# Feed forward: raw blocks of up and of the down projection in chunks of the large pool, only gate in the staging tiles, and the down sums in other PSUM banks

## The chip, the cores and the metric

The kernel runs on one core of one Trainium2 chip. The metric is device time in microseconds (us), from the start to the end of one execution. Lower is better.

## What is computed

Three residual blocks on one sequence of 512 rows with a model width of 1024. The first mixes attention and a gated delta rule; the second and the third are two layers of attention and feed forward (FFN). The change touches only the FFN, which runs once in each of these two layers:

```python
D_MODEL = 1024; SEQ = 512; D_FF = 2816; DEPTH_2 = 2

def swiglu_ffn(h, w_gate, w_up, w_down):
    g = jnp.einsum('bsd,df->bsf', h, w_gate)
    u = jnp.einsum('bsd,df->bsf', h, w_up)
    return jnp.einsum('bsf,fd->bsd', jax.nn.silu(g) * u, w_down)

def second_block(x, ...):
    for i in range(DEPTH_2):
        ...
        x = x + swiglu_ffn(rms_norm_2(x, ffn_norm[i]), w_gate[i], w_up[i], w_down[i])
    return x
```

Everything is float32. The width D_FF of 2816 is 22 blocks of 128 columns.

## The kernel before, in words

**Numbers.** Each float32 operand of a matmul is split into a rounded part (float32r) and a remainder: ScalarE casts the rounded part (`hi`), VectorE subtracts it from the original (`lo`), in `split` (L315). A product is then three matmuls, hi x hi, hi x lo, lo x hi (`mm3`). So a weight block has to be loaded, cast on ScalarE and subtracted on VectorE before TensorE has all that it needs. In the trace these are `whi` (L318) and `wlo` (L321).

**Tiling.** `ffn` (L2043) goes over 22 units, one for each block of 128 columns of gate and up. All activations lie feature first, so a result is 128 features x 512 rows.
- Units 0 to 3 are `plain`: gate (`pg`) and up (`pu`) are each 24 matmuls of 512 columns.
- Units 4 to 21 (`unit`) get gate and up together from 7 Strassen-like products instead of 8, each of 12 matmuls of 256 columns, into halves of three PSUM banks `sx`, `sy`, `sz`. `weights` (L2115) makes their stationary operands: gate itself for products 1 and 2, the sum of up's two halves (`s`, rounded `s1h` and `s1l`) for 5, a combination of gate and up for 6 and 3, and a difference made in up's own tile for 7 and 4. Product 4 of a unit is left pending, and issued in the next unit (`rest`). The products are issued in the order 1, 5, 4 of the unit before, 2, 6, 3, 7. The FFN's hidden block `m` is then split into `mh` and `ml` (`keep`).
- Units 4 to 19 carry a "fill" each: a part of the down projection. It takes 4 hidden blocks and two blocks of output features, 12 matmuls of 512 columns each into a bank `pd`; an add on VectorE (L600) then brings the sum into the residual `x`. The first half of a fill stands behind products 5 and 4, the second behind 6. The fill of unit 4 is issued ahead of its products.
- `down(16)` does the rest of the down projection, 8 x 18 matmuls.

**Memory.** Raw weights come through two staging tiles of 128 x 1024 (pool `wst`, tile name `st`). In a filled unit three loads go through them: gate (L2120), up (L2124), and the two halves of the down block (L2157). The rounded pairs `whi`, `wlo` have three places each, and every fourth pair goes into a place of its own. Chunks of 128 x 512 come from the pool `big` (57 places), which holds the activations, the hidden blocks and `s1`, `s1h`, `s1l`. PSUM has two banks of kind `acc`, five of kind `z` and one `o`; `sx` and `pd` use `acc`, `sy` and `sz` use `z`.

**What sets the order.** SyncE (SP) issues the loads. A scheduler at build time writes each engine's instructions in a fixed order: it goes by the order of the code, with the loads and the splits of `weights` and `fill` raised by a fixed priority (`high_priority`). A tile that is asked for waits until the last reader of its place is done. Since SP works through its own list in order, a load that waits for a place holds up all loads behind it. On TensorE a small driver (`Driver`) decides when the code goes from one stream to another; `self.free["acc"]` and `self.free["z"]` are its counts of free banks, which `release` returns.

Of the kernel before, what the change touches and what calls it, by code (L numbers as in the profile page):

```python
# [9 lines left out]
F32 = mybir.dt.float32  # L10
# [3 lines left out]
ALU = mybir.AluOpType  # L14
# [3 lines left out]
P = 128  # L18
T = 512
D = 1024  # L20
NC8 = 8
DFF = 2816
NFF = 22
# [145 lines left out]
class Net:  # L169
# [1873 lines left out]
    def ffn(self, x, R, l, nxt):  # L2043
# [11 lines left out]
        nc, ins, drv = self.nc, self.ins, self.drv  # L2055
# [35 lines left out]
        def plain(c, raw):  # L2091
            hh, ee = (R.h, R.ev) if raw else (h, ev_h)
            sg = self.work("sg")

            def evac_g(ps):
                if raw:
                    nc.vector.tensor_tensor(sg, ps, self.rfm, op=ALU.mult)
                    nc.scalar.activation(out=sg, in_=sg, func=AF.Silu)
                    nc.vector.tensor_tensor(sg, sg, self.rfm, op=ALU.mult)
                else:  # L2100
                    nc.scalar.activation(out=sg, in_=ps, func=AF.Silu)

            def evac_u(ps):
                m = self.work("m")
                nc.vector.tensor_tensor(m, ps, sg, op=ALU.mult)
                keep(c, m)
            yield from self.proj_fm([(ins["w_gate_2"][NFF * l + c], 8)], hh, evac_g, "pg", ee)
            yield from self.proj_fm([(ins["w_up_2"][NFF * l + c], 8)], hh, evac_u, "pu", ee)

        def keep(c, m):  # L2110
            mid[0][c], mid[1][c] = self.chunk(f"mh{c}", F32R), self.chunk(f"ml{c}", F32R)
            self.split(mid[0][c], mid[1][c], m)
            drv.set(evs[c], 2.5)

        def weights(c):  # L2115

            tt = lambda o, p, q, op: nc.vector.tensor_tensor(o, p, q, op=op)  # L2117
            with self.tc.high_priority(offset=self.woff):
                g = self.wst.tile([P, 1024], F32, tag="st", name="st")
                nc.sync.dma_start(out=g, in_=ins["w_gate_2"][NFF * l + c])  # L2120
                gh, gl = self.wpair()
                self.split(gh, gl, g)
                u = self.wst.tile([P, 1024], F32, tag="st", name="st")
                nc.sync.dma_start(out=u, in_=ins["w_up_2"][NFF * l + c])  # L2124
                s1 = self.chunk("s1")
                tt(s1, u[:, :T], u[:, T:], ALU.add)
                sh, sl = self.chunk("s1h", F32R), self.chunk("s1l", F32R)
                self.split(sh, sl, s1)

                tt(u[:, :T], g[:, :T], u[:, :T], ALU.subtract)  # L2130
                tt(g[:, :T], s1, g[:, :T], ALU.subtract)
                tt(g[:, T:], g[:, T:], g[:, :T], ALU.subtract)
                ch, cl = self.wpair()
                self.split(ch, cl, g)
                uh, ul = self.wpair()
                self.split(uh, ul, u)
            return {1: (gh, gl, 0), 2: (gh, gl, T), 5: (sh, sl, 0), 6: (ch, cl, 0), 3: (ch, cl, T),
                    7: (uh, ul, 0), 4: (uh, ul, T)}

# [12 lines left out]
        def fill(g, c):  # L2152

            with self.tc.high_priority(offset=self.woff):
                st = self.wst.tile([P, 1024], F32, tag="st", name="st")
                for i in range(2):
                    nc.sync.dma_start(out=st[:, T * i:T * i + T], in_=ins["w_down_2"][NC8 * l + c + i][:, T * g:T * g + T])  # L2157
                hi, lo = self.wpair()
                self.split(hi, lo, st)

            def one(i):
                yield self.free["acc"]
                acc = self.bank("acc", "pd")
                for j in range(4):
                    yield evs[4 * g + j]
                    cc = slice(T * i + j * P, T * i + (j + 1) * P)
                    self.mm3(acc, (hi[:, cc], lo[:, cc]), (mid[0][4 * g + j], mid[1][4 * g + j]), j == 0, j == 3)
                    yield 0
                part_x(c + i, acc)
                drv.release(self.free["acc"], 1.5)  # L2170
            return [one(0), one(1)]

        def unit(c, pending, fills):

            add = lambda o, p, q: nc.vector.tensor_tensor(o, p, q, op=ALU.add)  # L2175
            if fills and not pending:
                fills = fill(*fills)
                while fills:
                    yield from fills.pop(0)
            w = weights(c)  # L2180
            if fills:
                fills = fill(*fills)
# [64 lines left out]

        def stream():
            for c in range(4):
                yield from plain(c, c < RAW_UNITS)  # L2250
            pending = None
            for c in range(4, NFF):
                g = c // 4 - 1
                pending = yield from unit(c, pending, (g, 2 * (c % 4)) if g < 4 else None)
            yield from down(16, pending)
        drv.run([self.s_raw_end(R, tm=False), operands(), stream()])


# [109 lines left out]
```

## Time and profile before

| | |
|---|---|
| median of 3 runs | 2182.99 us (2180.08 to 2188.91) |
| the profiled execution's own time | 2191.84 us |
| its span in the profile | 2190.0 us |
| mean granted TensorE clock | 0.984 of full speed |
| busy share of the span | TensorE 96%, weight loads 85%, VectorE 67%, ScalarE 51%, GpSimd 5% |
| data moved | 181.93 MB, mean 83 GB/s |

The profile is of one execution; the times are of others. "Busy" for TensorE (PE) means that at least one matmul is under way. PEld are weight loads into TensorE, which overlap with matmuls; DVE is VectorE, ACT is ScalarE, POOL is GpSimd, SPq the queue of DMA issues on SyncE. `L302` is the line of the matmul in a helper that all products use, so groups on TensorE are told apart by their tiles.

### The profile page before, as it was taken

Reading aid. Unit: us, or ns where it says so; the run is one execution under the profiler, and the core shown is the slowest. Engines: PE = TensorE matmul, PEld = TensorE weight load, DVE = VectorE, ACT = ScalarE, POOL = GpSimd, SP = SyncE. Lnnn points to the kernel's source line nnn. Section 1 sums busy time; section 2 is a strip of 40 time slices with the busy share of each in tenths; the row PEclk is TensorE's granted clock in tenths of the full one; section 3 lists DMA queues with packets and bytes.
Section 4 is the critical chain, followed back from the end, with each engine's and each line's share of the span. In section 5 each row is a group of like instructions: output and inputs, shape, how many; then the busy total and the mean of one; then the engine's idle time right before and its main releaser. Section 6 shows DMA issues by size and latency. Waiting matters only on the chain.

```text
span 2190.0 us, 36607 instructions
## 1 busy us (share of the span) xinstructions
PE 2094.3 (96%) x14510; PEld 1851.3 (85%) x14510; DVE 1457.2 (67%) x2947; ACT 1112.6 (51%) x2227; POOL 117.2 (5%) x157
## 2 busy tenths in 40 slices
PE   7999999989999998999999999999999989999999
PEld 6798888879788877788878889988999877988887
DVE  8865865886442556755557777776677768766664
ACT  6556647555622355666655444444556644443432
POOL 2000100100000000000000000000111100000000
PEclk9999999999999999999999999999999999999999
DMA  4221121222334443011112233324211112232233
GB/s 157 70 81 50 46 74 50 59 80 64 100 101 140 149 156 104 20 49 49 58 47 89 75 100 102 101 87 118 76 59 59 59 53 73 90 104 87 90 94 106
DMA packets 78619, 181.93 MB, mean 83 GB/s; under 512 B 24688, under 2 KB 25328, under 8 KB 78448
## 3 DMA queue, kind: packets, MB, share of 16 engines
q1 hardware_dynamic: 77168, 175.40, 25.8%
q0 software_dynamic: 1280, 4.20, 0.6%
q8 instruction: 114, 1.87, 0.4%
q14 instruction: 57, 0.47, 0.1%
HBM read 170.13 MB, written 9.44 MB: 82 GB/s over the span
## 4 chain that ended last, share of the span: by engine, by line
PE 60%; DVE 20%; ACT 7%; DMA 6%; issue 3%; POOL 2%; SPq 0%; ACTq 0%; POOLq 0%; DVEq 0%
PE po L302 8%; PE pd L302 8%; PE pg L302 6%; DVE wlo L321 5%; PE sx L302 4%; PE pb L302 4%; ACT whi L318 3%; PE pz L302 3%; PE z L302 3%; PE pv L302 3%; PE sz L302 2%; DMA st<-w_up 2%; DMA st<-w_down 2%; PE wS L302 2%; DVE cacc L850 2%
## 5 line engine op out<-in xcount | busy, mean ns | idle before, releaser
L318 ACT CAST whi<-st 128x1024 fp32r<-128x1024 f32 (+1 forms) x331 | 341.3, 1039 | 484.3 <-DVE st L2117 72.2
L321 DVE TENSOR_TENSOR wlo<-st,whi 128x1024 fp32r<-128x1024 f32 (+1 forms) x331 | 398.4, 1210 | 220.6 <-ACT whi L318 216.4
L302 PE MATMUL pd<-mh,whi 128*128 128x512 f32 x352 | 145.3, 413 | 9.0 <-ACT whi L318 4.3
L302 PE MATMUL pd<-mh,wlo 128*128 128x512 f32 x352 | 140.4, 399 | 0.3 <-DVE wlo L321 0.3
L302 PE MATMUL pd<-ml,whi 128*128 128x512 f32 x352 | 139.2, 396 | 0.0
L302 PE MATMUL sx<-thi,wlo 128*128 128x256 f32 x432 | 122.3, 283 | 0.3 <-DVE wlo L321 0.3
L302 PE MATMUL sx<-thi,whi 128*128 128x256 f32 x432 | 122.3, 283 | 0.1
L302 PE MATMUL sx<-tlo,whi 128*128 128x256 f32 x432 | 121.9, 282 | 0.0
L302 PEld LDWEIGHTS pd<-mh,whi 128*128 128x128 f32 x352 | 66.9, 190 | 27.9 <-ACT whi L318 8.6
L600 DVE TENSOR_TENSOR x<-pd,x 128x512 f32<-128x512 f32 x80 | 54.9, 686 | 45.7 <-PE pd L302 45.3
L302 PEld LDWEIGHTS sx<-thi,whi 128*128 128x128 f32 x432 | 82.3, 190 | 1.6 <-DVE c L2175 0.3
L302 PEld LDWEIGHTS sx<-thi,wlo 128*128 128x128 f32 x432 | 82.3, 190 | 1.3 <-DVE wlo L321 0.5
L302 PEld LDWEIGHTS sx<-tlo,whi 128*128 128x128 f32 x432 | 82.2, 190 | 1.1
L302 PEld LDWEIGHTS pd<-mh,wlo 128*128 128x128 f32 x352 | 66.8, 190 | 14.9 <-DVE wlo L321 1.1
L302 PE MATMUL pv<-whi,rhi 128*128 128x256 f32 x256 | 76.0, 297 | 3.3 <-ACT tmq L1873 2.1
L302 PE MATMUL pz<-wlo,hhi 128*128 128x256 f32 x256 | 75.0, 293 | 4.1 <-DVE wlo L321 2.5
L302 PEld LDWEIGHTS pd<-ml,whi 128*128 128x128 f32 x352 | 67.0, 190 | 12.8 <-DVE ml L321 0.7
L302 PE MATMUL pz<-whi,hhi 128*128 128x256 f32 x256 | 76.4, 298 | 0.9 <-ACT cacc L846 0.9
L850 DVE SCALAR_TENSOR_TENSOR cacc<-craw,convw,cacc 128x510 f32<-128x510 f32 (+1 forms) x96 | 70.8, 747 | 7.6 <-ACT cacc L846 6.6
L302 PE MATMUL pz<-whi,hlo 128*128 128x256 f32 x256 | 75.1, 293 | 0.0
L302 PE MATMUL pv<-wlo,rhi 128*128 128x256 f32 x256 | 72.3, 282 | 0.0
L302 PE MATMUL pv<-whi,rlo 128*128 128x256 f32 x256 | 72.2, 282 | 0.0
(622 smaller groups left out, 6666.2 us busy)
## 6 DMA issues: line engine op xcount, KB each, us to landing
st<-w_gate SPq DMA_DIRECT2D x44, 512.0 KB, 3.6
st<-w_up SPq DMA_DIRECT2D x44, 512.0 KB, 3.6
st<-w_down SPq DMA_DIRECT2D x64, 256.0 KB, 2.9
st<-w_dn SPq DMA_DIRECT2D x24, 512.0 KB, 3.6
st<-w_out SPq DMA_DIRECT2D x24, 512.0 KB, 3.5
st<-w_down SPq DMA_DIRECT2D x16, 384.0 KB, 3.2
x<-xT SPq DMA_DIRECT2D x16, 256.0 KB, 6.0
st<-w_aq SPq DMA_DIRECT2D x8, 512.0 KB, 3.5
```

Of the source, the lines that this page charges most:

```text
L302: self.nc.tensor.matmul(out, lhsT=lhsT, rhs=rhs, start=start, stop=stop, skip_group_check=True)
L318: nc.scalar.copy(hi, src)
L321: nc.vector.tensor_tensor(lo, src, hi.bitcast(F32), op=ALU.subtract)
L600: self.nc.vector.tensor_tensor(x[c], ps, x[c], op=ALU.add)
L850: nc.vector.scalar_tensor_tensor(out=acc[:, a], in0=raw[:, b], scalar=w[:, s:s + 1], in1=acc[:, a], op0=ALU.mult, op1=ALU.add)
```

## The change

Gate alone goes through the staging tiles. Up is loaded as two halves into two chunks of `big` (`ust`), each with a DMA of its own. The two halves of the down block go into two chunks of `big` as well (`dst`), except in the first fill, (0, 0), which keeps a staging tile. The splits of up's difference and of the down block are made in two halves of 512 columns instead of one of 1024. The down sums `pd` take banks of kind `z` instead of `acc`. And the first fill is built ahead of unit 3 and handed to unit 4 as ready generators. Tiles, numbers and matmuls are otherwise the same.

```diff
--- before.py
+++ after.py
@@ -2120,20 +2120,23 @@
                 nc.sync.dma_start(out=g, in_=ins["w_gate_2"][NFF * l + c])
                 gh, gl = self.wpair()
                 self.split(gh, gl, g)
-                u = self.wst.tile([P, 1024], F32, tag="st", name="st")
-                nc.sync.dma_start(out=u, in_=ins["w_up_2"][NFF * l + c])
+                u = []
+                for i in range(2):
+                    u.append(self.chunk("ust"))
+                    nc.sync.dma_start(out=u[i], in_=ins["w_up_2"][NFF * l + c][:, T * i:T * i + T])
                 s1 = self.chunk("s1")
-                tt(s1, u[:, :T], u[:, T:], ALU.add)
+                tt(s1, u[0], u[1], ALU.add)
                 sh, sl = self.chunk("s1h", F32R), self.chunk("s1l", F32R)
                 self.split(sh, sl, s1)
 
-                tt(u[:, :T], g[:, :T], u[:, :T], ALU.subtract)
+                tt(u[0], g[:, :T], u[0], ALU.subtract)
                 tt(g[:, :T], s1, g[:, :T], ALU.subtract)
                 tt(g[:, T:], g[:, T:], g[:, :T], ALU.subtract)
                 ch, cl = self.wpair()
                 self.split(ch, cl, g)
                 uh, ul = self.wpair()
-                self.split(uh, ul, u)
+                for i in (1, 0):
+                    self.split(uh[:, T * i:T * i + T], ul[:, T * i:T * i + T], u[i])
             return {1: (gh, gl, 0), 2: (gh, gl, T), 5: (sh, sl, 0), 6: (ch, cl, 0), 3: (ch, cl, T),
                     7: (uh, ul, 0), 4: (uh, ul, T)}
 
@@ -2152,31 +2155,32 @@
         def fill(g, c):
 
             with self.tc.high_priority(offset=self.woff):
-                st = self.wst.tile([P, 1024], F32, tag="st", name="st")
+                hi, lo = self.wpair()
+                both = self.wst.tile([P, 1024], F32, tag="st", name="st") if (g, c) == (0, 0) else None
                 for i in range(2):
-                    nc.sync.dma_start(out=st[:, T * i:T * i + T], in_=ins["w_down_2"][NC8 * l + c + i][:, T * g:T * g + T])
-                hi, lo = self.wpair()
-                self.split(hi, lo, st)
+                    st = self.chunk("dst") if both is None else both[:, T * i:T * i + T]
+                    nc.sync.dma_start(out=st, in_=ins["w_down_2"][NC8 * l + c + i][:, T * g:T * g + T])
+                    self.split(hi[:, T * i:T * i + T], lo[:, T * i:T * i + T], st)
 
             def one(i):
-                yield self.free["acc"]
-                acc = self.bank("acc", "pd")
+                yield self.free["z"]
+                acc = self.bank("z", "pd")
                 for j in range(4):
                     yield evs[4 * g + j]
                     cc = slice(T * i + j * P, T * i + (j + 1) * P)
                     self.mm3(acc, (hi[:, cc], lo[:, cc]), (mid[0][4 * g + j], mid[1][4 * g + j]), j == 0, j == 3)
                     yield 0
                 part_x(c + i, acc)
-                drv.release(self.free["acc"], 1.5)
+                drv.release(self.free["z"], 1.5)
             return [one(0), one(1)]
 
         def unit(c, pending, fills):
 
             add = lambda o, p, q: nc.vector.tensor_tensor(o, p, q, op=ALU.add)
             if fills and not pending:
-                fills = fill(*fills)
-                while fills:
-                    yield from fills.pop(0)
+                for f in fills:
+                    yield from f
+                fills = None
             w = weights(c)
             if fills:
                 fills = fill(*fills)
@@ -2247,11 +2251,13 @@
 
         def stream():
             for c in range(4):
+                if c == 3:
+                    first = fill(0, 0)
                 yield from plain(c, c < RAW_UNITS)
             pending = None
             for c in range(4, NFF):
                 g = c // 4 - 1
-                pending = yield from unit(c, pending, (g, 2 * (c % 4)) if g < 4 else None)
+                pending = yield from unit(c, pending, first if c == 4 else (g, 2 * (c % 4)) if g < 4 else None)
             yield from down(16, pending)
         drv.run([self.s_raw_end(R, tm=False), operands(), stream()])
 
```

The next pieces show the built order of an engine before and after, from the same place of the program. A name's number tells one tile from another; a bracket lists the semaphores that the instruction waits for (`DVE` for VectorE, `Activation` for ScalarE, `PE` for TensorE, `DMAHW` for DMA queues).

SP, the loads of two successive filled units in the second FFN, before: gate, up, and the two halves of down, unit by unit.

```order
L2120 DMA st_20558<-w_gate_2 128x1024 [waits DMAHW4_49,DVE_49]
L2124 DMA st_20564<-w_up_2 128x1024 [waits DMAHW6_49,DMAHW5_49,DVE_49]
L2157 DMA st_20583<-w_down_2 128x512 [waits DMAHW7_49,DVE_49]
L2157 DMA st_20583<-w_down_2 128x512
L2120 DMA st_20722<-w_gate_2 128x1024 [waits DMAHW0_49,DVE_49]
L2124 DMA st_20728<-w_up_2 128x1024 [waits DMAHW2_49,DMAHW1_49,DVE_49]
L2157 DMA st_20747<-w_down_2 128x512 [waits DMAHW3_49,DVE_49]
```

SP at such a place after the change: `ust` are up's halves, `dst` those of down; tiles 20888 to 20917 belong to one unit, 21053 to 21061 to the next, 21224 to the one after.

```order
L2120 DMA st_21053<-w_gate_2 128x1024 [waits DMAHW4_49,DVE_49]
L2126 DMA ust_20888<-w_up_2 128x512 [waits DMAHW5_49,PE_49]
L2126 DMA ust_20890<-w_up_2 128x512 [waits DMAHW6_49]
L2162 DMA dst_20913<-w_down_2 128x512 [waits DMAHW7_49,PE_49]
L2162 DMA dst_20917<-w_down_2 128x512 [waits DMAHW0_49]
L2120 DMA st_21224<-w_gate_2 128x1024 [waits DMAHW1_49,DVE_49]
L2126 DMA ust_21059<-w_up_2 128x512 [waits DMAHW2_49]
L2126 DMA ust_21061<-w_up_2 128x512 [waits DMAHW3_49]
```

Every load of before waits for VectorE; after it, the gate load of a unit stands ahead of the up and down loads of the unit before, and those wait for TensorE or for nothing but the DMA queue.

VectorE, from the add of product 2 (`sg<-sy`) to the split of the next unit's sum `s1`, second FFN, before.

```order
L2175 TENSOR_TENSOR sg_20605<-sy_20653,c12_20603 128x256 [waits PE_49]
L321 TENSOR_TENSOR wlo_20587<-st_20583,whi_20586 128x1024 [waits DMAHW2_49,DMAHW1_49,Activation_49]
L321 TENSOR_TENSOR wlo_20725<-st_20722,whi_20724 128x1024 [waits DMAHW3_49,Activation_49]
L600 TENSOR_TENSOR x2_9684<-pd_20639,x2_9684 128x512 [waits PE_49]
L2117 TENSOR_TENSOR s1_20730<-st_20728 128x512 [waits DMAHW4_49]
L2175 TENSOR_TENSOR sg_20605<-sz_20608,c12_20603 128x256 [waits PE_49]
L2117 TENSOR_TENSOR st_20728<-st_20722,st_20728 128x512 [waits DVE_49]
L321 TENSOR_TENSOR s1l_20733<-s1_20730,s1h_20732 128x512 [waits Activation_49]
```

VectorE from the same add after the change.

```order
L2179 TENSOR_TENSOR sg_20936<-sy_20984,c12_20934 128x256 [waits PE_49]
L2117 TENSOR_TENSOR s1_21063<-ust_21059,ust_21061 128x512 [waits DMAHW3_49,DMAHW2_49]
L321 TENSOR_TENSOR wlo_21056<-st_21053,whi_21055 128x1024 [waits DMAHW4_49,Activation_49]
L321 TENSOR_TENSOR s1l_21066<-s1_21063,s1h_21065 128x512 [waits Activation_49]
L2117 TENSOR_TENSOR ust_21059<-st_21053,ust_21059 128x512
L2117 TENSOR_TENSOR st_21053<-s1_21063,st_21053 128x512 [waits DVE_49]
L600 TENSOR_TENSOR x2_9771<-pd_21011,x2_9771 128x512 [waits PE_49]
L2117 TENSOR_TENSOR st_21053<-st_21053 128x512 [waits DVE_49]
L2179 TENSOR_TENSOR sg_20936<-sz_20939,c12_20934 128x256 [waits PE_49]
```

The sum `s1` of the next unit stood behind two splits of 1024 columns, one of them the fill's, and the fill's add; now it stands directly behind the add of product 2.

TensorE, second FFN, before: the end of a fill's second half and the start of product 5 of the next unit.

```order
L302 MATMUL pd_20680<-mh7_20471,whi_20586 128x512
L302 MATMUL pd_20680<-ml7_20472,whi_20586 128x512
L302 MATMUL pd_20680<-mh7_20471,wlo_20587 128x512
L302 MATMUL sz_20772<-thi_19449,s1h_20732 128x256 [waits Activation_49]
L302 MATMUL sz_20772<-tlo_19450,s1h_20732 128x256
L302 MATMUL sz_20772<-thi_19449,s1l_20733 128x256 [waits DVE_49]
```

TensorE, second FFN, after: the end of product 4 of the unit before and the start of the fill.

```order
L302 MATMUL sx_20750<-thi_19841,whi_20734 128x256
L302 MATMUL sx_20750<-tlo_19842,whi_20734 128x256
L302 MATMUL sx_20750<-thi_19841,wlo_20735 128x256
L302 MATMUL pd_20970<-mh4_20111,whi_20911 128x512 [waits Activation_49]
L302 MATMUL pd_20970<-ml4_20112,whi_20911 128x512
L302 MATMUL pd_20970<-mh4_20111,wlo_20912 128x512
```

In the second FFN the units after the change keep the order of the code (1, 5, 4 of the unit before, first half of the fill, 2, 6, second half, 3, 7) and no group is split; in the first FFN the groups of product 2, of product 6 and of the fill are still cut into pieces that alternate. In both FFNs the first fill's matmuls stand between those of unit 3.

## Rows read from the trace of the kernel before

**Rows 1.** The page: busy us (share of the span) and instructions of each engine.

```profile
PE 2094.3 (96%) x14510; PEld 1851.3 (85%) x14510; DVE 1457.2 (67%) x2947; ACT 1112.6 (51%) x2227; POOL 117.2 (5%) x157
```

**Rows 2.** Chain of work in order, first FFN: start, us, engine, tile, line, instructions.

```profile
1355.69 2.29 PE pd L302 x10
...
1358.93 2.85 PE pd L302 x12
...
1363.21 2.86 PE sx L302 x24
...
1371.53 2.29 PE pd L302 x10
```

**Rows 3.** Timeline of PE: start, us, instruction; product 2 of units 4 and 21.

```profile
1227.24 0.28 PE L302 MATMUL sy<-hhi,whi 128*128 128x256 f32 x1
...
1492.00 0.28 PE L302 MATMUL sy<-hhi,whi 128*128 128x256 f32 x1
...
1868.29 0.28 PE L302 MATMUL sy<-hhi,whi 128*128 128x256 f32 x1
...
2143.27 0.28 PE L302 MATMUL sy<-hhi,whi 128*128 128x256 f32 x1
```

**Rows 4.** Waits of PE (us, count, longest), units of the first and second FFN.

```profile
PE pd L302 <- ACT whi L318: 2.5, 4, 1.7
PE pd L302 <- DVE x L600: 1.7, 2, 1.2
...
PE sz L302 <- ACT s1h L318: 6.1, 5, 2.2
...
PE pd L302 <- DVE x L600: 1.0, 4, 0.3
```

**Rows 5.** Chain, then timeline [idle before, releaser], around one wait, second FFN.

```profile
2101.68 4.87 DMA st<-w_up
...
2107.30 0.62 ACT L318 CAST s1h<-s 128x512 fp32r<-128x512 f32 x1 [3.16 <-DVE s L2117]
...
2107.97 0.38 PE L302 MATMUL sz<-thi,s1h 128*128 128x256 f32 x1 [2.22 <-ACT s1h L318]
```

**Rows 6.** Waits of SP's queue, whole first FFN: us, count, longest.

```profile
SPq L2157 <- DVE wlo L321: 143.3, 16, 10.4
```

**Rows 7.** Windows: us, busy PE, PEld, DVE, ACT, POOL, clock, DMA share, GB/s.

```profile
1972.00:1976.00 4.00, 4.00 (x13) 3.13 (x12) 2.62 (x6) 1.04 (x1) 0.00 (x0) 0.57 0.00 0
1976.00:1980.00 4.00, 4.00 (x34) 3.95 (x33) 1.82 (x2) 0.65 (x2) 0.00 (x0) 1.00 0.13 28
```

**Rows 8.** Groups by shape, units of the first FFN: busy, mean ns, idle before.

```profile
L321 DVE TENSOR_TENSOR wlo<-st,whi 128x1024 fp32r<-128x1024 f32 x68 | 81.7, 1223 | 27.3 <-ACT whi L318 27.2
...
L321 DVE TENSOR_TENSOR s1l<-s,s1h 128x512 fp32r<-128x512 f32 x18 | 12.4, 691 | 0.0
...
L318 ACT CAST s1h<-s 128x512 fp32r<-128x512 f32 x17 | 10.6, 622 | 24.8 <-DVE s L2117 24.7
...
L2175 DVE TENSOR_TENSOR c<-sx,c 128x256 f32<-128x256 f32 x18 | 7.5, 418 | 0.8 <-PE sx L302 0.8
```

**Rows 9.** Timeline of ACT and PE at the start of a fill, first FFN.

```profile
1353.02 1.05 ACT L318 CAST whi<-st 128x1024 fp32r<-128x1024 f32 x1 [0.95 <-PE sx L302]
...
1354.12 0.50 PE L302 MATMUL pd<-mh,whi 128*128 128x512 f32 x1
```

**Rows 10.** Windows, filled units of the second FFN, columns as above.

```profile
2020.00:2060.00 40.00, 38.34 (x256) 34.90 (x255) 28.97 (x44) 15.60 (x24) 0.00 (x0) 1.00 0.31 91
```

**Rows 11.** Timeline of SP: one pair of down loads.

```profile
1349.01 0.80 SPq L2157 DMA_DIRECT2D st<-w_down  x2
```

**Rows 12.** The page: DMA issues, KB each, median us from issue to landing.

```profile
st<-w_up SPq DMA_DIRECT2D x44, 512.0 KB, 3.6
st<-w_down SPq DMA_DIRECT2D x64, 256.0 KB, 2.9
```

**Rows 13.** Timeline of PE in unit 3, first FFN.

```profile
1210.90 0.50 PE L302 MATMUL pg<-hhi,whi 128*128 128x512 f32 x1 [0.44 <-ACT hhi L318]
```

## Prediction

> **What bounds the kernel now.** I read the page's engine line first: TensorE has matmuls in flight for 96% of a span of 2190.0 us [rows 1]. Its ends are modelled, so this says only that the other engines matter where TensorE waits for them. The built order of all five engines is the same, before and after, up to the first feed forward (FFN), and again from the end of its last projection to the start of the second FFN; only the two FFN stretches can change. So I measured those.
>
> A Strassen unit (units 4 to 21 of each FFN) issues 7 products of 12 matmuls of 256 columns, 84 in all; units 5 to 19 also carry a "fill", 24 matmuls of 512 columns. The chain of work in the first FFN shows 24 narrow matmuls in 2.86 us and 12 wide ones in 2.85 us [rows 2]. That gives a floor of 84/24 x 2.86 = 10.01 us for the products and 24/12 x 2.85 = 5.70 us for the fill: 15.71 us for a filled unit. The same chain has a stretch in which this is nearly reached: the same point of two successive units stands at 1355.69 and 1371.53, 15.84 us apart [rows 2].
>
> Then the whole stretch. The first matmul of product 2 (tile sy) of unit 4 and of unit 21 stand at 1227.24 and 1492.00 in the first FFN, at 1868.29 and 2143.27 in the second [rows 3]: 264.76 and 274.98 us for 17 units' products and 15 fills. The floor is 17 x 10.01 + 15 x 5.70 = 255.7 us. So 9.1 and 19.3 us, 28.4 together, are above it. **This is the most that the change can win inside the units.** The list of waits says who is late: in the first FFN the fill's weights (`whi`, 2.5 us) and the add that frees the bank of the down sum (`x`, 1.7); in the second above all `s1h`, the rounded sum of up's halves, 6.1 us in 5 waits, and `x` again, 1.0 [rows 4]. Those numbers are smaller than mine because the modelled ends cover part of each gap.
>
> One such wait read backwards: up's load is issued at 2101.68, takes 4.87 us, the cast of the sum `s` starts at 2107.30, and product 5 at 2107.97 after 2.22 us of idle TensorE [rows 5]. Why was up's load so late? The queue that issues loads waits for `wlo`, the last reader of a staging tile: in the first FFN 143.3 us in 16 waits at the down load (L2157) alone [rows 6]. Three loads a unit go through two staging tiles. One of these waits cost twice: behind it the granted clock is 0.57 over 4 us, the lower of its two levels (1.2 of 2.4 GHz) for most of that time, and the window has 13 matmuls where the next one has 34 [rows 7]. That loss is part of the 19.3 us.
>
> **The change, part by part.**
>
> *Up and down in chunks of the large pool.* The built order shows gate loads running one unit further ahead, and up's and down's issued behind them, one after the other. Let 0 be the start of product 1 in a filled unit of the second FFN, with TensorE at the floor: 5 at 1.43, the last unit's 4 at 2.86, first half of the fill 4.29, 2 at 7.14, 6 at 8.57, second half 10.0, 3 at 12.85, 7 at 14.28, next unit 15.71. VectorE follows in its new order with the durations of [rows 8]: 0.42 us for 256 columns, 0.69 for 512, 1.22 for 1024; ScalarE 0.62 and 1.05.
> - Up's sum for the next unit comes behind product 2's add: 8.57 + 0.2 + 0.42 = 9.2, ending 9.9, its cast 10.5, `wlo` of gate 11.1, `s1l` 11.8. Product 5 needs it at 15.71 + 1.43 = 17.1: a margin of 5.3 us where now it is late.
> - The loads for it are released when the present unit's combined gate block is split, at about 1.4. Five issues of some 0.40 (0.80 for a pair, [rows 11]) and a landing of 3.6 [rows 12] put the last at about 7, two microseconds before VectorE wants it and over 8 before TensorE would stop.
> - The combined block: sums, the second add, product 3's add, cast and split end at about 17.1; product 6 needs it at 24.3.
> - The fill's two casts end at about 17.2, its splits at 18.5; it is needed at 20.0: margin 1.5 us.
>
> So no wait is left in a unit of the second FFN but fractions where a sum of the last unit is used at once (units 8, 12, 16: 0.2 each). I leave 0.04 a unit.
>
> In the first FFN the new order splits product 6 around the first two fill matmuls. The fill's pair of weight tiles is the one that product 4 frees, so its cast starts when product 4 ends. Before, that cast started when a product ended, took 1.05 us, and the fill's first matmul stood 1.10 us behind its start [rows 9], all of it under other matmuls but the 0.13 us by which the 15.84 exceed the floor. Now the cast is half as long, 0.62, behind six narrow matmuls, 0.71. I keep 0.13 a unit.
>
> *Two splits where there was one.* Up and down each have two of 0.69 instead of one of 1.22, on ScalarE 0.62 twice instead of 1.05: +0.32 us of VectorE and +0.38 of ScalarE a unit. VectorE then has 12 x 0.69 + 2 x 1.22 + 5 x 0.42 = 12.8 of 15.7 us. It has 28.97 of 40 us in a stretch of the second FFN now [rows 10], so it stays off the path; cost nothing, and if that cover were gone 30 x 0.32 = 10 us.
>
> *Two loads for up.* A load of 256 KB lands 2.9 us after its issue, one of 512 KB after 3.6 [rows 12]: with 0.40 for an issue the pair is there 0.4 + 2.9 = 3.3 us after the first issue, no later than one large load. The Trainium skill speaks against such a cut: "DMA: Bandwidth & Descriptors", section Bandwidth, wants loads batched to 1 MiB or more, and its section on the anatomy of one DMA gives each about 2.0 us whatever its size. By that, with the 2.0 us on the path of each of 34 units, the sum would be 68 us longer (an estimate from that page). The rows above disagree, because the second load's wait runs beside the first's, and the sum goes by them.
>
> *Down sums in `z` banks.* Removes the waits of the fill for the add (`x`, 1.7 and 1.0 us [rows 4]) and of `sx` for it. Four of five `z` banks are used in a unit, and the fifth frees long before product 5. In the 28.4 already.
>
> *The first fill ahead of unit 3.* Its wide matmuls now stand between those of unit 3, where TensorE waits 0.44 us for `hhi` in the first FFN [rows 13]. With as much again for `hlo` and the same in the second FFN that is 1.8 us, an estimate from this one row; taken as 1.6. In return units 4 and 5 start with both up sums behind the first fill's two adds on VectorE; by the durations of [rows 8] product 6 of unit 4 waits some 0.6 us for its split and the fill of unit 5 some 1.1 for its cast: 1.7 us an FFN. Bounds: nothing, and about 4 if each of the two stalls is as long as the one in [rows 5].
>
> **The sum.** First FFN 9.1 - 15 x 0.13 - 1.7 = 5.4; second 19.3 - 15 x 0.04 - 1.7 = 17.0; unit 3: 1.6. Together 24 us of the profiled execution's own 2191.84: 2168. That execution is 8.85 us above the median of the runs, 2182.99, and the trace can't say where. If all of it lies in waits that go, the median loses only 15; if none, 24. I take 22: 2161 us. The bounds of the terms: 28.4 + 1.8 won at best (2153), and 5.4 + 15 x 0.04 lost to extra VectorE waits and 4.6 more at the start of the FFNs, with the 9 us, leave about 8 (2175).
>
> **Rivals.**
> 1. *Staging moves the wait only part of the way* (chance 0.18). The pairs of rounded weights stay at four a unit, and each cast waits for TensorE to leave a pair. For it: the 1.5 us margin of the fill is thin, and [rows 9] shows a cast that starts the moment a product ends. Against it: `s1h` has no such pair. If 0.3 to 0.5 us a unit stay, 9 to 15 of the 22 us are lost: 2170 to 2176.
> 2. *Head of the queue: slower* (0.07). Gate's load now stands ahead of up's and waits for a staging tile; everything behind it waits too. It decides once up lands over 8 us later than worked out, 15.5 us after product 1. Each unit then stops as in [rows 5], 2.2 us, and some fall to the lower clock: ten such units cost 22 us and eat the gain; all thirty would give 2183 + 66 - 22 = 2227. Against it: the gate load waits for a split that is 7 us ahead of its use. The cut loads belong here too, and the rows speak against them.
> 3. *Nothing to see* (0.11). The stretches above the floor are gaps between units that no load causes, such as the turn from narrow to wide matmuls; or the change of order gives back in the first FFN what the second wins. Time 2174 to 2190. Against: the 15.84 us unit shows that the turns fit in the floor.
>
> **How the numbers follow.** My forecast has 0.64, with a range of its own of 2152 to 2169. About 0.5% (11 us) is what a measurement here tells from no change, so faster means below 2172. Faster: 0.64 and 0.11 of rival 1, 0.75. Same: 0.07 of rival 1 and rival 3, 0.18. Slower: 0.07. The range that leaves out no more than two in ten is 2150 to 2177.
>
> **What would show it.** In the changed profile the sy matmuls of units 4 and 21 should stand 259 us apart in the first FFN and 258 in the second; the waits on `s1h` and on `x` should be gone, and no stretch of the second FFN should show a clock below 0.9. The loading queue's long waits should stand at gate (L2120), not at down. VectorE's idle before `m` (the end of product 4) should remain, a sign that it has slack. Wrong would be: waits of `sz` on `s1h` in most units (rival 2), waits of `pd` on `whi` of 0.3 us and more in each (rival 1), or stretches as long as now with no wait listed (rival 3).

## The result and the profile after

The changed kernel takes 2160.3 us (median of 4 runs, 2157.81 to 2161.41) where the kernel before took 2181.53: a ratio of 0.9896 (95% interval 0.9869 to 0.9922), 21 us or 1.0% faster. The forecast was 2161.

Start with the page's engine line, the counterpart of [rows 1]. TensorE's busy share is 96% again: that number alone would have shown nothing.

```profile
PE 2077.3 (96%) x14510; PEld 1845.1 (86%) x14510; DVE 1463.8 (68%) x3015; ACT 1114.7 (52%) x2295; POOL 117.3 (5%) x157
```

The timeline of TensorE at the four instants of [rows 3] shows where the time came from: product 2 of units 4 and 21, first and second feed forward (FFN).

```profile
1222.51 0.28 PE L302 MATMUL sy<-hhi,whi 128*128 128x256 f32 x1
...
1480.20 0.28 PE L302 MATMUL sy<-hhi,whi 128*128 128x256 f32 x1
...
1853.92 0.28 PE L302 MATMUL sy<-hhi,whi 128*128 128x256 f32 x1
...
2110.51 0.28 PE L302 MATMUL sy<-hhi,whi 128*128 128x256 f32 x1
```

The 17 units take 257.69 us in the first FFN (264.76 before) and 256.59 in the second (274.98). The list of TensorE's waits in these two stretches, against [rows 4], has lost `x`; of `s1h` and `whi` one wait each is left, in units 4 and 5, where all the rest stand too:

```profile
PE sx L302 <- DVE wlo L321: 0.8, 1, 0.8
PE pd L302 <- ACT whi L318: 0.6, 1, 0.6
...
PE sz L302 <- DVE s1l L321: 0.5, 1, 0.5
PE sz L302 <- ACT s1h L318: 0.4, 1, 0.4
PE sx L302 <- DVE wlo L321: 0.2, 1, 0.2
```

One unit of the second FFN, from the timeline of VectorE, ScalarE and TensorE. `s` is the sum of the next unit's up, and the `sz` matmul is where product 5 needs it; `dst` is the down block, and `pd` the fill that needs it.

```profile
2011.56 0.68 DVE L2117 TENSOR_TENSOR s<-ust 128x512 f32<-128x512 f32 x1
...
2012.93 0.62 ACT L318 CAST s1h<-s 128x512 fp32r<-128x512 f32 x1
...
2013.58 0.69 DVE L321 TENSOR_TENSOR s1l<-s,s1h 128x512 fp32r<-128x512 f32 x1
...
2017.87 1.13 ACT L318 CAST whi<-dst 128x512 fp32r<-128x512 f32 x2
...
2019.14 1.29 DVE L321 TENSOR_TENSOR wlo<-dst,whi 128x512 fp32r<-128x512 f32 x2
...
2019.49 0.28 PE L302 MATMUL sz<-thi,s1h 128*128 128x256 f32 x1
...
2022.36 0.40 PE L302 MATMUL pd<-mh,whi 128*128 128x512 f32 x1
```

The sum's last split ends at 2014.27, 5.2 us ahead of product 5 (forecast 5.3); that of the fill at 2020.43, 1.9 ahead of the fill (forecast 1.5). SP's longest group of waits in the first FFN is longer than in [rows 6], 218.8 us for 143.3, but stands at gate's load now, which is a unit ahead, and the list above has no wait behind unit 5 that could come from it. The window of the second FFN that answers to [rows 10] has the full clock and TensorE busy throughout, and no stretch of 1 us in either FFN has a granted clock below 0.95.

```profile
SPq L2120 <- DVE wlo L321: 218.8, 17, 24.2
```
```profile
2000.00:2040.00 40.00, 40.00 (x285) 37.69 (x285) 30.77 (x51) 18.98 (x33) 0.00 (x0) 1.00 0.34 113
```

### The profile page after: what moved, and what is told of

Its sections match the earlier page's. It is cut to its first block, busy times and chain, and to the rows that moved or that the text cites. A ratio compares the mean times of both kernels' runs of the same rounds, so it can differ in the third digit from the quotient of the medians.

```text
span 2156.1 us, 36812 instructions
## 1 busy us (share of the span) xinstructions
PE 2077.3 (96%) x14510; PEld 1845.1 (86%) x14510; DVE 1463.8 (68%) x3015; ACT 1114.7 (52%) x2295; POOL 117.3 (5%) x157
## 4 chain that ended last, share of the span: by engine, by line
PE 78%; DVE 12%; ACT 5%; issue 2%; POOL 2%; DMA 1%; SPq 0%; POOLq 0%; DVEq 0%; ACTq 0%
PE pd L302 11%; PE sx L302 9%; PE po L302 9%; PE pg L302 8%; PE sz L302 5%; PE pb L302 4%; PE pv L302 3%; PE pz L302 3%; PE z L302 3%; PE sy L302 2%; PE pu L302 2%; DVE wlo L321 2%; PE wS L302 2%; DVE cacc L850 2%; PE sb_q L302 2%
## 5 line engine op out<-in xcount | busy, mean ns | idle before, releaser
L318 ACT CAST whi<-st 128x1024 fp32r<-128x1024 f32 (+2 forms) x267 | 274.0, 1031 | 538.0 <-issue 111.7
L321 DVE TENSOR_TENSOR wlo<-st,whi 128x1024 fp32r<-128x1024 f32 (+2 forms) x267 | 319.0, 1198 | 162.7 <-ACT whi L318 158.4
L302 PE MATMUL pd<-mh,whi 128*128 128x512 f32 x352 | 140.2, 398 | 2.0 <-DVE m L2219 1.2
```

The costliest lines, as they stand in the source:

```text
L302: self.nc.tensor.matmul(out, lhsT=lhsT, rhs=rhs, start=start, stop=stop, skip_group_check=True)
L318: nc.scalar.copy(hi, src)
L321: nc.vector.tensor_tensor(lo, src, hi.bitcast(F32), op=ALU.subtract)
```

## The experiments

The table gives every run in the same measure, from the timeline of TensorE: from unit 0's first matmul to product 2 of unit 4, then the 17 units (each for the first and second FFN), then the whole of both FFNs from unit 0 to the last matmul of `down(16)`. "Rest" is the span without the FFNs. A median's ratio is to runs of the kernel before on the same chip; the other columns are from one profiled execution each. Times in us.

| run | median, ratio (95%) | to unit 4 | 17 units | both FFNs | rest |
|---|---|---|---|---|---|
| before | 2181.53 | 54.96, 54.94 | 264.76, 274.98 | 733.3 | 1456.6 |
| before_again | one run, 2185.97 | 54.95, 54.97 | 264.57, 271.94 | 730.2 | 1453.9 |
| changed | 2160.30, 0.9896 (.9869 to .9922) | 53.77, 53.11 | 257.69, 256.59 | 703.5 | 1452.6 |
| after_again | 2159.26, 0.9882 (.9861 to .9903) | 53.79, 53.11 | 257.71, 256.72 | 703.6 | 1456.6 |
| up_alone | 2165.01, 0.9902 (.9875 to .9928) | 53.99, 54.01 | 258.62, 260.33 | 709.3 | 1456.0 |
| down_alone | 2169.88, 0.9922 (.9894 to .9950) | 55.03, 55.07 | 258.01, 260.62 | 712.3 | 1456.1 |
| banks_alone | 2214.49, 1.0138 (1.0113 to 1.0162) | 53.47, 53.53 | 297.84, 269.12 | 760.3 | 1453.2 |
| undo_up | 2170.35, 0.9929 (.9904 to .9954) | 53.61, 53.45 | 259.85, 260.30 | 713.7 | 1458.3 |
| undo_down | 2161.88, 0.9888 (.9865 to .9912) | 53.78, 53.11 | 258.35, 257.47 | 705.1 | 1454.9 |
| undo_banks | 2165.44, 0.9903 (.9878 to .9928) | 53.63, 53.75 | 256.99, 263.14 | 709.8 | 1455.2 |
| undo_early | 2159.81, 0.9880 (.9859 to .9901) | 54.56, 53.24 | 257.71, 256.69 | 704.5 | 1452.0 |
| third_tile | 2171.22, 0.9937 (.9920 to .9954) | 54.91, 54.92 | 257.90, 262.92 | 713.2 | 1459.7 |
| four_loads | 2163.78, 0.9892 (.9870 to .9915) | 53.78, 53.14 | 257.69, 259.61 | 707.6 | 1455.7 |
| whole_groups | 2157.72, 0.9871 (.9853 to .9888) | 53.26, 53.12 | 256.33, 256.40 | 701.5 | 1448.2 |

The FFNs repeat to 0.2 us in the changed kernel and to 3.2 in the one before. The rest varies by 10 us, though its built order is the same in all runs but third_tile. So small differences are read from the FFN column, and those of 1 or 2 us, from one execution each, are no more than likely.

That column holds the same matmuls in every run. The two to the left of it do not quite: by the timeline, 24 narrow matmuls (256 columns) of units 4 and 5 stand ahead of product 2 of unit 4 in the kernel before, in down_alone, banks_alone, undo_up and third_tile; 26 in the first FFN and 16 in the second in the changed kernel, undo_down, undo_early and four_loads; 16 and 16 in whole_groups, 15 and 14 in up_alone, 14 and 14 in undo_banks. Each moves 0.12 us from one column to the other. "With the same work" below means that this is taken out: the changed kernel's 17 units then take 257.9 and 255.6, its stretches to unit 4 53.5 and 54.1.

### One part alone

up_alone and down_alone take that part of the diff over and leave the others (the splits of the part in halves included). banks_alone:

```diff
-                yield self.free["acc"]
-                acc = self.bank("acc", "pd")
+                yield self.free["z"]
+                acc = self.bank("z", "pd")
...
-                drv.release(self.free["acc"], 1.5)
+                drv.release(self.free["z"], 1.5)
```

> Only up's raw halves go into chunks of the large pool; down stays in the staging tiles, its sums in acc banks, the first fill where it was. Theory A (what held the units up was up's load, late because three loads a unit pass two staging tiles): 14 us or more of the 21 are won, ratio 0.9935 or less, and the waits of product 5 on s1h are gone from the second FFN. Theory B (only all loads but gate's out of the staging tiles help; two loads through two tiles are as late as three): under 5 us, ratio above 0.9977. Theory C (the gain is that of the down sums' banks, through the order in which whole groups are issued): under 5 us.

> Only the raw down halves go into chunks (the first fill's excepted); up keeps its staging tile. Theory A: up's load no longer stands behind down's waits, and as only gate and up share two tiles it is in time: 10 us or more, ratio 0.9954 or less; the queue of loads has its long waits at up or gate. Theory B: under 5 us. Theory C: under 5 us.

> Only the down sums move from acc to z banks. Theory A: at most the 2.7 us of listed waits on the add x in the units of both FFNs, ratio 0.9985 or more, and s1h is waited for as before. Theory B: the same. Theory C: 7 us or more, ratio 0.9968 or less.

up_alone wins 21 us of its chip's 2186.26 and down_alone 16, in the FFNs 22 and 19 of 28 (against the mean of the two profiles of before, 731.7). Together they would be 41: they remove the same thing, and either nearly suffices. That is theory A; B falls. The waits on `s1h` are gone from the second FFN in up_alone, and in down_alone the queue's long waits stand at gate and up, as A said. In both, and in third_tile below, the sum `s` also stands earlier in VectorE's order than before, no longer behind the fill's split; a place to land in and this order come together, and no run separates them.

For banks_alone all theories were wrong. It was to win 7 us or at most 2.7, and loses 28. TensorE's waits in its first FFN:

```profile
PE pd L302 <- ACT whi L318: 12.5, 15, 2.3
PE sx L302 <- DVE wlo L321: 9.7, 18, 0.8
```

Its chain of work shows what the weights are late for:

```profile
1398.54 1.06 ACT whi L318
...
1399.62 1.24 DVE wlo L321
...
1400.88 0.33 SPq L2157
...
1401.26 2.98 DMA st<-w_down
...
1404.31 1.05 ACT whi L318
...
1405.41 0.73 PE pd L302 x2
...
1409.86 2.75 PE pd L302 x12
1412.61 1.45 PE sx L302 x12
1414.06 1.44 PE sz L302 x12
...
1415.52 0.02 ACT c L2191
...
1415.79 1.06 ACT whi L318
```

A ring, but not of loads alone: a cast and a split free a staging tile, SP issues the down load, which lands and is cast; TensorE then does the fill with product 2 between its pieces and products 1 and 5 of the next unit, and behind the copy of product 5 ScalarE comes to the next cast. One turn, from 1398.54 to 1415.79, takes 17.25 us: 6.8 to the end of the down block's cast, 10.1 on TensorE, the rest between them. TensorE's own work for a unit is some 15.6. In the timeline of this FFN its order is 1, 5, 4 of the unit before, 6, 3, 7, and only then the fill and product 2; so product 6 stands close behind the split that frees the tile (the waits of `sx` for `wlo`), and the fill waits for a down load that starts behind the same split. SP waits 168.5 us at that load for a tile. So three loads through two tiles are part of the cause here too, and undo_down below, with these banks and one load fewer through the tiles, is within 1.5 us of the changed kernel in the FFNs; the order that came with the banks put the waits where TensorE feels them.

### The kernel before once more

> The kernel before, profiled once more, to see how far its first profile, 10 us above the median of its runs, is typical. If the extra time lay in the units of the second FFN (theory D): product 2 of units 4 and 21 stand 262 to 270 us apart there instead of 275, and in the first FFN 262 to 265 as before. If it lay elsewhere (theory E): 273 to 277 again, and the stretch ahead of the first FFN is shorter than 1172 us by 3 us or more.

Neither expectation held. The first FFN is the same to 0.2 us; the second's units are at 271.94, between the two; the rest is 2.7 us shorter. Of the 5.9 us between the two profiles 3.2 lie in the FFNs, and 3.0 of these in the second's units, where the granted clock falls once and not twice. The wait ahead of the stretch at 0.57 in [rows 7] comes again in before_again, nearly as long, and the clock stays:

```profile
1971.65 0.38 PE L302 MATMUL sz<-thi,s1h 128*128 128x256 f32 x1 [1.74 <-ACT s1h L318]
```
```profile
1968.32 0.38 PE L302 MATMUL sz<-thi,s1h 128*128 128x256 f32 x1 [1.67 <-ACT s1h L318]
```
```profile
1969.00:1973.00 4.00, 4.00 (x26) 3.57 (x25) 3.79 (x7) 1.05 (x1) 0.00 (x0) 1.00 0.00 0
```

### One part undone

after_again is the changed kernel; the other runs put that part of the diff back.

> The changed kernel once more, on the chip and in the rounds of the three that each undo one part of it. All theories: 2155 to 2165 us; product 2 of units 4 and 21 stand 257 to 259 us apart in the first FFN and 256 to 258 in the second.

> The changed kernel with the raw down block back in a staging tile and its split in one piece. Theory A (one load less through the two tiles is enough): within 5 us of the changed kernel, the 17 units at most 262 us in either FFN. Theory F (down sums in z banks let the scheduler place the fill's matmuls earlier, and that hurts wherever the fill's weights still come through the staging queue, as where the banks were changed alone): 10 us or more slower than the changed kernel, with waits of pd on whi in the first FFN.

> The changed kernel with raw up back in a staging tile, loaded by one transfer, its difference split in one piece. Theory A: within 5 us of the changed kernel. Theory F: no loss either, since the fill's weights are not in that queue. Theory G (what is needed is above all that up's load does not wait for a tile): 8 us or more slower, with waits of sz on s1h.

> The changed kernel with the down sums back in acc banks. Theory A with the listed waits on the add x: 1 to 4 us slower than the changed kernel. Theory F: the banks bring nothing by themselves, within 2 us. Theory C (banks are the main thing): 7 us or more slower, which the run with the banks alone speaks against.

after_again came as expected. undo_down loses 1.5 us in the FFNs: A holds, and F falls, since the fill's weights come through the staging queue here with z banks and the list has one wait for them, 1.1 us. It takes all three loads in the queue for the banks to hurt.

undo_up loses 10.1 us in the FFNs, more than A allows, but not by G's wait: `s1h` is waited for twice in the second FFN, 0.4 us in all. 4.1 us are lost behind the units of the second FFN, where `down(16)` waits 1.6 us for its first weights, and a TensorE that was busy 2.12 of 4 us goes on at a clock of 0.64, 13 matmuls in 4 us:

```profile
2128.00:2132.00 4.00, 2.12 (x11) 1.40 (x10) 1.62 (x3) 2.09 (x3) 0.00 (x0) 0.93 0.15 54
2132.00:2136.00 4.00, 4.00 (x13) 3.17 (x12) 1.45 (x3) 0.83 (x1) 0.00 (x0) 0.64 0.66 197
```

The other 6 are in the units, 1.9 and 4.7 with the same work, less 0.5 ahead of unit 4. In the second FFN the built order now cuts the fill's first half behind its first matmul, around product 4.

undo_banks loses 6.3 us, and not by waits for `x`, of which the list has none left. With the same work, the units of the second FFN lose 6.3 and those of the first win 2.1, while 2.2 go ahead of unit 4, where the first fill stands behind unit 3's matmuls again and TensorE waits for `hhi` and `hlo` as before the change. In the second FFN product 2 is cut behind its first matmul, and two gaps stand in each unit, in the timeline of TensorE:

```profile
1931.00 0.28 PE L302 MATMUL sy<-hhi,whi 128*128 128x256 f32 x1
1931.31 0.39 PE L302 MATMUL sx<-thi,whi 128*128 128x256 f32 x1
...
1933.32 0.28 PE L302 MATMUL sy<-hhi,wlo 128*128 128x256 f32 x1
1933.61 0.47 PE L302 MATMUL pd<-mh,whi 128*128 128x512 f32 x1
```

Narrow matmuls are otherwise 0.12 us apart; here they are 0.31 and 0.29. A unit takes 16.05 us instead of 15.5 to 15.6. Why TensorE pauses at such a cut is not shown. The wait for `hhi` in unit 3, first FFN:

```profile
1209.85 0.50 PE L302 MATMUL pg<-hhi,whi 128*128 128x512 f32 x1 [0.38 <-ACT hhi L318]
```

So the banks are worth 6 us with up and down out of the staging tiles, through the order, and cost 28 with both in them. With down alone out they bring nothing: undo_up's FFNs take 713.7, those of down_alone, in acc banks, 712.3.

### The first fill, a third tile, more transfers, whole groups

undo_early puts the first fill back into unit 4. third_tile is the kernel before with

```diff
-POOLS = dict(big=57, tmp=9, sm=4)
+POOLS = dict(big=55, tmp=9, sm=4)
...
-POOLS2 = dict(w3=1)
+POOLS2 = dict(w3=1, us=1)
...
-                u = self.wst.tile([P, 1024], F32, tag="st", name="st")
+                u = self.us.tile([P, 1024], F32, tag="us", name="us")
```

four_loads is the changed kernel with

```diff
-                    nc.sync.dma_start(out=u[i], in_=ins["w_up_2"][NFF * l + c][:, T * i:T * i + T])
+                    for k in (0, 256):
+                        nc.sync.dma_start(out=u[i][:, k:k + 256], in_=ins["w_up_2"][NFF * l + c][:, T * i + k:T * i + k + 256])
```

and whole_groups the changed kernel with

```diff
             pending = None
+            if l == 0:
+                self.nw += 2
             for c in range(4, NFF):
...
+            if l == 0:
+                self.nw += 2
             yield from down(16, pending)
```

> The changed kernel with the first fill built in unit 4 again. By the prediction's term the early fill gives back as much as it brings: the time stays within 3 us of the changed kernel. If it brings what it seemed to in the profile (unit 0 to product 2 of unit 4: 53.8 and 53.1 us in the changed kernel, 55.0 before), that stretch is 54 to 55 us here in both feed forwards and 2 to 3 us are lost. Theory J (it is the z banks that let the fill in among unit 3's matmuls, since the run with the banks alone had 53.5 there): the stretch stays at 53 to 54.

> The kernel before with a third tile of 128 x 1024 for raw up alone, loaded by one transfer and split in one piece, paid for by two places of the large pool (55 instead of 57). Theory A (places in staging are what was short, chunks and halves only one way to have more): as with up alone in chunks, 14 us or more faster than before, ratio 0.9935 or less. Theory H (halves and paired loads matter by themselves): under 7 us, ratio above 0.9968.

> The changed kernel with up's raw block loaded in four transfers of 128 KB instead of two of 256. By the margin of 5 us that up's sum has, two more issues of 0.4 us cost nothing by themselves: within 5 us of the changed kernel, no waits of sz on s1h of over 0.5 us. If a transfer's wait stood on the path of the queue each time, two more per unit at 2.9 us would cost over 100 us.

> The changed kernel with the count that gives every fourth pair of rounded weights its own place moved on by two ahead of unit 4 of the first feed forward, and by two again behind unit 21. There the fill's matmuls then are issued as whole groups, as in the second one. Theory K (pieces that alternate between 256 and 512 columns cost the 0.23 us by which a unit of the first, 15.73, is above one of the second, 15.50): 17 units in 253 to 257 us instead of 257.7, 1 to 4 us in all, ratio to before 0.985 to 0.989. If the pieces cost nothing: 257 to 259 us.

undo_early: 1.0 us more in the FFNs, 0.8 of it ahead of unit 4 in the first and 0.1 in the second. The stretch there is 53.24 in the second, as J said, and 54.56 in the first, as the other theory said; but banks_alone, without the early fill, had 53.5 in both, and in undo_early the fill's matmuls stand between those of unit 3 and no wait for `hhi` or `hlo` is listed, where undo_banks, with the early fill, has both. So J holds: the banks let the fill in. The stalls of units 4 and 5 are here as well, so they are not the price of building the fill early:

```profile
1225.04 0.39 PE L302 MATMUL sx<-thi,wlo 128*128 128x256 f32 x1 [0.76 <-DVE wlo L321]
...
1232.89 0.50 PE L302 MATMUL pd<-mh,whi 128*128 128x512 f32 x1 [0.64 <-ACT whi L318]
```

third_tile: 14.7 us of its chip's 2185.89 by the medians, and a ratio of 0.9937, a hair short of A's 0.9935; in the FFNs 18.6 of 28. It has neither halves nor pairs of loads, so H falls: one more place to land in is enough for most of the gain. Its rest is the longest of all, 1459.7, and in another built order; but its profiled execution has a mean granted clock of 0.984, as has that of undo_up with 1458.3, so that whether the two places fewer in the large pool cost something is not shown.

four_loads: no wait of TensorE on up is longer than in the changed kernel, in the second FFN:

```profile
PE sz L302 <- DVE s1l L321: 0.5, 1, 0.5
PE sz L302 <- ACT s1h L318: 0.4, 1, 0.4
```

The FFNs take 4.1 us more, 3.0 of it in the units of the second, where the built order cuts the fill behind its first matmul as in undo_up, and 0.9 behind the units of the first. The "DMA: Bandwidth & Descriptors" page of the Trainium skill (section Anatomy of one DMA — SWDGE (gpsimd) path) gives a transfer issued from GpSimd a fixed 2.0 us, most of it waiting for completion. These loads are issued from SyncE; with the same 2.0 on the path twice more in each of 36 units that would be 144 us, an estimate from that page. This run shows none of it on the path: the four loads of a unit are issued some 0.45 us apart, and all have landed 5.2 us after the first issue (median), where the changed kernel's two take 4.8. The profile's page, landing of each:

```profile
ust<-w_up SPq DMA_DIRECT2D x144, 128.0 KB, 3.6
```

whole_groups: both FFNs take 701.5 us, 2.0 less than in the changed kernel: with the same work the units of the first take 2.5 less, and 0.7 more go ahead of unit 4. The two instants in its timeline:

```profile
1216.97 0.28 PE L302 MATMUL sy<-hhi,whi 128*128 128x256 f32 x1
...
1473.31 0.28 PE L302 MATMUL sy<-hhi,whi 128*128 128x256 f32 x1
```

Its units run as those of the second FFN do, in turns of 15.50, 15.50, 15.06 and 16.29, a mean of 15.59, not the 15.50 that K counted with. K's range held, at a price of 0.14 a unit and not 0.23. Its median is the shortest of all kernels here, but 2157.7 cannot be told from the changed kernel's.

## Why the prediction was right

**The bound.** The step "three loads a unit go through two staging tiles" held: each of three ways to give one load another place (up_alone, down_alone, third_tile) wins 18.6 to 22.4 us of 28 in the FFNs. The signs held as well: no stretch of the second FFN below a clock of 0.9, the queue's long waits at gate, `x` gone from the lists. What a fall of the clock costs was read too high: [rows 7] sets 13 matmuls against 34 of another mix, and the same place at full clock has 26 in before_again.

**The sum.** Forecast were 24 us of the profiled execution. Its FFNs lost 733.3 - 703.5 = 29.8, so 5.8 were missed:
- Units of the first FFN, 5.4 forecast, 7.1 measured; second, 17.0 and 18.4; with the same work 6.8 and 19.4. The floor of 15.71 us was too high. It was read from one group of [rows 2], where 12 wide matmuls took 2.85 us. The chain of the changed kernel, second FFN, has less:

```profile
2012.62 2.75 PE pd L302 x12
2015.37 1.43 PE sz L302 x12
2016.80 2.85 PE sx L302 x24
...
2022.52 2.73 PE pd L302 x12
```

  84/24 x 2.85 + 2.75 + 2.73 = 15.46, and units of 15.50 stand in the trace (their mean is 15.59). In the first FFN 15.71 + 0.13 was forecast and 15.73 measured.
- Unit 3, 1.6 forecast; the stretch to unit 4 lost 1.2 and 1.8, with the same work 1.4 and 0.9. The term was near, its cause was wrong: undo_early and undo_banks show that the waits for `hhi` and `hlo` go with the banks, whether the fill is built ahead of unit 3 or not.
- 1.3 us behind unit 21 of the second FFN (42.58 to 41.24) were in no term. They come with up out of the staging tiles: by the same instants every run with up in a staging tile has 42.5 or more there, every other 41.4 or less.

**The stalls in units 4 and 5.** Forecast 0.6 and 1.1 us, 1.7 together, in each FFN. The list for the first has two waits there, 0.8 and 0.6: right in kind, in the other order of size. In the second FFN it is above all product 5 of unit 4 that waits, 0.4 and 0.5, and product 6 only 0.2; there, too, the groups of units 4 and 5 are cut into pieces. The reason given, the early fill, was wrong: undo_early has the same stalls, and undo_banks, which has the early fill, neither of the first FFN's. What makes them was not tried.

**From the sum to the median.** 22 was taken, on the thought that the 8.85 us by which the first profile lay above the median might lie in waits that go. Only 3.0 of the 5.9 us by which the second profile was shorter lay in the units. With 28 us in the FFNs, the medians fell by 21 and 27 in two comparisons. So that 2161 is met to 1 us is luck: the sum was 5.8 short, the discount of 2 for the median had no row behind it, and the other comparison gave 27. The range was the claim, and its lower end is not what its own terms give: 24 - 6.0 - 4.6 - 9 is 4.4, 2179, not 2175.

**The banks.** "Removes the waits of the fill for the add" was the wrong mechanism. Put back, they cost 6.3 us with no wait for `x` listed, and alone they lose 28. In the kernel before the waits on `x` are listed; what the banks brought the changed kernel is another order on TensorE and the first fill among unit 3's matmuls. The term was counted in the 28.4 and so did no harm to the number.

**Two loads for up, and the splits in halves.** They cost nothing that shows, as forecast: four loads put no wait on the path, and VectorE's busy share went from 67% to 68%. But "no later than one large load" was wrong: the pair was to be there 3.3 us after its first issue, and takes 4.8 (median of 36, 4.2 to 6.1), where one large load took 3.6 [rows 12]. 2.9 was counted for a landing; issued behind gate's load and one another, they took, by the profile's page,

```profile
ust<-w_up SPq DMA_DIRECT2D x72, 256.0 KB, 4.2
dst<-w_down SPq DMA_DIRECT2D x60, 256.0 KB, 4.7
```

and the margin of 5 us hid it. The 68 us that the forecast set beside its sum did not come; the 2.0 us behind them are, as said at four_loads, those of another issuing engine. VectorE still waits for product 4 ahead of `m`, 18.9 us in the second FFN's units, the sign of slack that was named.

**The rivals.** Rival 2 (gate at the head of the queue) did not come: its waits are there, 218.8 us, but a unit ahead of the need. Rival 1 (casts that start when a product ends) foretold 0.3 to 0.5 us a unit; left are 0.14 in the first FFN, 15.73 against 15.59, and these went with the cut groups in whole_groups. Rival 3 was wrong for the loads, but its turn from narrow to wide is real: against the changed kernel whole_groups wins 2.0 us and undo_banks loses 6.3, with TensorE in another order and no listed wait to account for it.

## What to carry to other kernels

Count the loads of one round against the places that they land in, and follow the ring of load, cast, split and next load through every engine that it passes. Where it is longer than the bottleneck engine's work for a round, try giving one load a place of its own; here that won most of the gain, and which load it was mattered little. Where a scheduler writes the order, try each part of an edit alone and undone: the banks lost 28 us alone and won 6 in company. Read a floor from several groups, and from the shortest of them. And when runs are compared between two instants, count the instructions between them: the order may have moved some across.

## What the runs showed of the hardware

Parts of the program whose instructions stand in the same order took 1448 to 1458 us in different executions, where two executions of the changed kernel's FFNs agree to 0.2. The granted clock goes with it: whole_groups' profiled execution has a mean of 0.989 and the 1448.2, undo_up's 0.984 and the 1458.3. Among runs of one kernel it is the same: undo_banks took 2157.84 us at 0.992 and 2164.4 to 2166.8 at 0.987 to 0.988, undo_up 2163.82 at 0.990 and 2170.3 to 2173.8 at 0.984 to 0.987.

Whether the clock falls behind a wait differs from execution to execution. In undo_up TensorE was busy 2.12 of 4 us, with one wait of 1.6, and the next 4 us had a granted clock of 0.64, between its two levels (1.2 and 2.4 GHz) and nearer the lower. Behind the wait of 1.74 us shown above the kernel before has 13 matmuls in 4 us at 0.57, and before_again, behind 1.67, has 26 at 1.00. Between the FFNs the same transpose (`otr`) stands behind 2.46 us of wait in both the kernel before and up_alone, and the next whole 4 us have 0.57 in the one and 1.00 in the other. In the changed kernel's FFNs, where no listed wait is above 0.8 us, no fall shows.

Loads issued close behind one another overlap, but each takes longer: 256 KB landed in 2.9 us in the kernel before [rows 12], and in 4.2 and 4.7 behind a gate load of 512 KB and one another.
